# Dilated attention on one core: each compute engine's instructions issued in the order in which the program writes them

## The chip, the cores and the metric

The kernel runs on one core of one Trainium2 chip. Of the core's engines TensorE (PE in the profile) multiplies matrices and transposes, ScalarE (ACT), VectorE (DVE) and GpSimd (POOL) compute element by element, and SyncE (SP) issues most of the transfers between HBM and the on-chip memory SBUF. TensorE writes its results into PSUM, from where ScalarE and VectorE read them. Each engine takes its instructions from a queue of its own, in the order in which the compiler has put them there, and an instruction waits at the head of its queue until the semaphores that it names have been raised.

The metric is the device time of one execution of the program in microseconds (us), the median over runs. Lower is better.

## What is computed

The reference is two transformer blocks, one behind the other, over 2048 positions of width 1024. The change touches one stage of the first block, a dilated attention with 8 heads of width 64. Cut to what matters:

```python
DIL_PATTERNS = ((128, 1), (512, 4), (2048, 16))

def dilated_branch(q, k, v, slopes, window, dilation):
    r = window // (2 * dilation)
    ...
    s = jnp.einsum('bnqche,bnkche->bnchqk', qs, kw).astype(jnp.float32) * scale + bias
    s = jnp.where(mask, s, MASK_VALUE)
    m = jnp.max(s, axis=-1, keepdims=True)
    e = jnp.exp(s - m)
    l = jnp.sum(e, axis=-1, keepdims=True)
    o = jnp.einsum('bnchqk,bnkche->bnqche', e.astype(v.dtype), vw)
    ...
    return o, lse

def dilated_attention(q, k, v, slopes):
    outs, lses = [], []
    for window, dilation in DIL_PATTERNS:
        o, lse = dilated_branch(q, k, v, slopes, window, dilation)
        ...
    w = jax.nn.softmax(jnp.stack(lses, axis=0), axis=0)
    return jnp.sum(w[..., None] * jnp.stack(outs, axis=0), axis=0)
```

A query attends to the keys within 64 positions (the first pattern), and to keys at distances that are multiples of 4 and of 16 (the other two). The three results are merged by their softmax denominators.

## The kernel before

The program is a sequence of stages: the first projections (`phase_a`), a differential attention (`phase_b1`), the dilated attention (`phase_b2`), output projection and gate (`phase_c`), and the second block (`phase_d`, `phase_e`). The framework in which it is written takes the traced instructions with their dependencies, plays them through a timing model of its own, and so chooses for each engine an order of issue. Where several instructions are ready in that model, the one that the program writes first goes first. An instruction that the model takes to be ready can so be put ahead of one that the program wrote earlier.

`phase_b2` treats two kinds of tiles for each of the 8 heads, 16 tiles of 128 queries of each kind. A natural tile ("nat") holds neighbouring positions and does the first pattern against 256 keys. A residue tile ("res") holds positions of one residue modulo 4 and does the second and third pattern together, against 384 or 512 keys. One loop runs over `n` from 0 to 146. In each turn it writes pieces of several tiles, each at its own distance behind `n` (the constants `LB`, `LN`, `LEAD`, `DN`, `DR`). The order in which a turn writes them is this (the number of a piece's TensorE instructions in brackets):

- `scores_nat`, where `n` is even: scores of two nat tiles [4] (L563), VectorE adds the bias and takes the minimum, once for each tile (L566), ScalarE takes the exponential, once for each (L569)
- `scores_res`: scores of one res tile [2] (L590), VectorE (L593), ScalarE (L595)
- `trans_nat`, where `n` is odd: transposes [4] (L603), ScalarE copies them out of PSUM (L606), GpSimd splits them into a high and a low part (L610, L611)
- `trans_res`: transposes of a tile whose scores lie 4 turns back [3 or 4] (L622), ScalarE writes the high part (`d_ph`, L624), VectorE the low part (`d_pl`, L625), which reads what ScalarE wrote
- `back_nat`, where `n % 4 == 1`, and `back_res`, where `n % 4 == 3`: an attention output is transposed back [4] (L649), VectorE sums its two halves (L650)
- `pv_nat`, where `n % 4 == 0` [10] (L637), and `pv_res`, where `n % 4` is 1 or 2 [4 each] (L733): weights times values. ScalarE then copies the sum out of PSUM (`d_ta`, L643), at `n % 4 == 0` and `n % 4 == 2`

The res tiles of four turns have 512, 512, 384 and 384 keys, for `n % 4` of 0, 1, 2 and 3.

Once for each head some more is written. At `n = 16 h + 21` `back_nat` stores the head's nat results to HBM (L656, `d_o` to `s_o`) by a transfer on ScalarE's queue. At `n = 16 h + 33` `load_merge` loads them again in the order of the res tiles (L660, `s_o` to `d_a`), on ScalarE's queue too. It must wait until the store has landed. At `n = 16 h + 38` `weights` works out the merging factors from what was loaded: nine small VectorE instructions (L685 to L695, `d_mm` first) around two small ScalarE ones (L688, L689). For the last head these two come sooner. The merge itself goes to GpSimd piece by piece in the turns behind (`later`). `load_qk`, `load_vn`, `load_vr` and `double_k` fetch the operands of the next head, by SyncE's transfers, two ScalarE and some GpSimd instructions.

Of the kernel before, what the change touches and what calls it, by code (L numbers as in the profile page):

```python
# [1 line left out]

# [458 lines left out]
        rsqrt_dve(nc, fp, ssq, 128, ssq)  # L461


LB = 4
LN = 3
LEAD = 3
# [6 lines left out]
def phase_b2(tc, c, scr, nat_bias, res_bias, res_two):  # L473
    nc = tc.nc
    NS = 8 * NT
    with (
# [76 lines left out]
        def scores_nat(n):  # L553
            h, t = divmod(n, NT)
            q, k, _, _ = hd[h]
            if t == 0:
                o1s[h] = op1.tile([P, NT, 66], F32, name="d_o1")
            ml = o1s[h][:, t:t + 2, 64:66]
            ps = ps_n.tile([P, 2, 256], F32, name="d_sn")
            en = tp.tile([P, 2, 256], F32, name="d_en", bufs=3)  # L560
            for u in range(2):
                for i in range(2):
                    nc.tensor.matmul(ps[:, u], q[:, (t + u) * P:(t + u + 1) * P],  # L563
                                     k[i][:, (t + u) * P:(t + u) * P + 256], start=i == 0, stop=i == 1)
            for u in range(2):
                nc.vector.tensor_tensor_reduce(en[:, u], ps[:, u], nb[h % 2], 1.0, 3.0e38, ALU.add, ALU.min,  # L566
                                               ml[:, u, 0:1])
            for u in range(2):
                nc.scalar.activation(en[:, u], en[:, u], AF.Exp, bias=ml[:, u, 0:1], scale=-1.0,  # L569
                                     accum_out=ml[:, u, 1:2])  # L570
            en_[n] = en
# [5 lines left out]
        def scores_res(n):  # L577
            h, t = divmod(n, NT)
            q, k, _, _ = hd[h]
            if t == 0:  # L580
                m2s[h] = [sp.tile([P, NT], F32, name=nm, bufs=3) for nm in ("d_m2", "d_l2")]
            g4, s0 = divmod(t, 4)
            cls = 4 * s0 + g4
            m2, l2 = m2s[h][0][:, cls:cls + 1], m2s[h][1][:, cls:cls + 1]
            qr = q.rearrange("p (j r g) -> p j g r", r=P, g=4)[:, s0, g4]
            ps = ps_r.tile([P, 512], F32, name="d_sr")
            lo, hi = span(s0)
            for i in range(2):
                kr = k[i][:, 64:S + 64].rearrange("p (b g u) -> p g b u", g=4, u=16)[:, g4, lo // 16:hi // 16]
                nc.tensor.matmul(ps[:, lo:hi], qr, kr, start=i == 0, stop=i == 1)  # L590
            er = tp.tile([P, 512], F32, name="d_er")
            off = (3 - s0) * P
            nc.vector.tensor_tensor_reduce(er[:, lo:hi], ps[:, lo:hi], rb[h % 2][:, off + lo:off + hi], 1.0,  # L593
                                           3.0e38, ALU.add, ALU.min, m2)
            nc.scalar.activation(er[:, lo:hi], er[:, lo:hi], AF.Exp, bias=m2, scale=-1.0, accum_out=l2)  # L595
            er_[n] = er

        def trans_nat(n):
            en = en_.pop(n)
            pt = pt_n.tile([P, 2, 2, P], F32, name="d_tn")  # L600
            for u in range(2):
                for j in range(2):
                    nc.tensor.transpose(pt[:, u, j], en[:, u, j * P:(j + 1) * P], c["id"])  # L603
            t = n % 4
            pn = up.tile([P, 2, 2, P], F32, name="d_pn")
            nc.scalar.activation(pn, pt, AF.Copy)  # L606
            if t == 0:
                pn_[n // 4] = [pp.tile([P, 4, 2, P], F32R, name=nm) for nm in ("d_nh", "d_nl")]
            nh, nl = pn_[n // 4]
            nc.gpsimd.tensor_scalar(nh[:, t:t + 2], pn, 1.0, 1.0, ALU.mult, ALU.mult)  # L610
            nc.gpsimd.tensor_sub(nl[:, t:t + 2], pn, nh[:, t:t + 2].bitcast(F32))  # L611
# [45 lines left out]

        def load_merge(h):
            a1 = op.tile([P, NT, 66], F32, name="d_a1")
            nc.scalar.dma_start(a1.rearrange("r (j g) w -> r j (g w)", g=4),  # L660
                                scr["o1"][h].rearrange("(j r g) w -> r j (g w)", r=P, g=4))
            sz = op.tile([P, NT, 64], F32, name="d_sz")
            for j in range(4):
                nc.sync.dma_start(sz[:, 4 * j:4 * j + 4], by_rows(scr["sz"][:, 512 + 64 * h:576 + 64 * h], j))
            mrg[h] = [a1, sz]
# [9 lines left out]
        def weights(h):  # L675
            a1, sz = mrg.pop(h)
            o2 = o2s[h]
            m2, l2 = m2s.pop(h)
            m1, l1 = a1[:, :, 64], a1[:, :, 65]

            def small(nm):
                return sp.tile([P, NT], F32, name=nm, bufs=2)

            mm, d1, d2, ll, lt = (small(nm) for nm in ("d_mm", "d_d1", "d_d2", "d_ll", "d_lt"))
            nc.vector.tensor_tensor(mm, m1, m2, ALU.min)  # L685
            nc.vector.tensor_sub(d1, mm, m1)
            nc.vector.tensor_sub(d2, mm, m2)
            nc.scalar.activation(d1, d1, AF.Exp)  # L688
            nc.scalar.activation(d2, d2, AF.Exp)  # L689
            nc.vector.tensor_mul(ll, l1, d1)  # L690
            nc.vector.tensor_mul(lt, l2, d2)
            nc.vector.tensor_add(ll, ll, lt)
            nc.vector.reciprocal(ll, ll)
            nc.vector.tensor_mul(d1, d1, ll)
            nc.vector.tensor_mul(d2, d2, ll)  # L695
            av = a1[:, :, 0:64]
            sd = op.tile([P, NT, 64], F32, name="d_sd", tag="d_o2") if h == 7 else None
            hs = (slice(0, NT // 2), slice(NT // 2, NT))

            def scale(x, ap, w):  # L700
                nc.gpsimd.tensor_mul(ap[:, x], ap[:, x], w[:, x].unsqueeze(2).broadcast_to([P, NT // 2, 64]))

            if h == 7:
                nc.gpsimd.tensor_mul(sd, sz, d2.unsqueeze(2).broadcast_to([P, NT, 64]))
                nc.vector.tensor_mul(av, av, d1.unsqueeze(2).broadcast_to([P, NT, 64]))
                nc.vector.tensor_mul(av, av, sz)

                def tail():
                    nc.vector.tensor_mul(o2, o2, sd)
                    nc.vector.tensor_add(av, av, o2)  # L710
                    store_y(h, av)

                later.append(tail)
                return
            later.extend([
                *[lambda x=x: scale(x, av, d1) for x in hs],
                *[lambda x=x: scale(x, o2, d2) for x in hs],
                *[lambda x=x: nc.gpsimd.tensor_add(av[:, x], av[:, x], o2[:, x]) for x in hs],
                *[lambda x=x: nc.gpsimd.tensor_mul(av[:, x], av[:, x], sz[:, x]) for x in hs],
                lambda: store_y(h, av),  # L720
            ])
# [23 lines left out]
        for h in range(2):  # L745
            load_qk(h)
            load_vn(h)
            load_vr(h)
        for n in range(NS + LEAD + LB + 12):
            r = n - LEAD  # L750
            if n < NS and n % 2 == 0:
                scores_nat(n)
            if 0 <= r < NS:
                scores_res(r)
            m = n - LN
            if m % 2 == 0 and 0 <= m < NS:
                trans_nat(m)
            if 0 <= r - LB < NS:
                trans_res(r - LB)
            m = n - LN - DN  # L760
            if m % 4 == 0 and 0 <= m - 1 < NS:
                back_nat(m - 1)
            if m % 4 == 3 and 0 <= m < NS:
                pv_nat(m)
            for h in range(8):
                at = NT * (h + 1) + LN + DN + (BACK if h < 7 else 3)
                if n == at:
                    load_merge(h)
            m = r - LB - 4 - DR
            if 0 <= m and m % 4 == 2 and m < NS:  # L770
                back_res(m // NT, (m % NT) // 4)
            if 0 <= m < NS and m % 4 < 2:
                for kt in ((1, 2), (0, 3))[m % 4]:
                    pv_res(m // NT, (m % NT) // 4, kt)
            for h in range(8):
                if n == NT * (h + 1) + (WT if h < 7 else LEAD + LB + DR + 3):
                    weights(h)
            for f in later[:1 if n < NS else 2]:
                f()
            del later[:1 if n < NS else 2]  # L780
            h, t = divmod(n, NT)
            if 1 <= h < 7:
                if t == LEAD + 1:
                    load_qk(h + 1)
                if t == LN + DN + 1:
                    load_vn(h + 1)
                if t == LEAD + LB + DR + 2:
                    load_vr(h + 1)
                if t >= 8:
                    double_k(h + 1, t - 8)  # L790


def split_w(nc, dst, raw, gain=None, lo_eng=None):
# [580 lines left out]
```

## Time and profile before

| | |
|---|---|
| median of 3 runs | 3005.81 us (3000.62 to 3008.73) |
| the profiled execution, its own time | 2996.59 us |
| its span in the profile | 2994.8 us |
| mean granted TensorE clock | 0.985 |
| the stage that the change touches | from about 1320 to about 1712 us of the span |

The span is the time between the first and the last instruction of the profiled execution; its own time is 1.8 us longer. The granted clock is TensorE's clock as a share of 2.4 GHz; its two levels are 1.0 and 0.5 (2.4 and 1.2 GHz), and a number between them is a mean over a stretch.

### The profile page before, as it was taken

What the parts mean: (1) busy time and instruction counts of PE and PEld (TensorE: products, weight loads), DVE (VectorE), ACT (ScalarE), POOL (GpSimd) and SP (SyncE); (2) the same over time, 40 slices, a digit from 0 to 9 for tenths busy, and PEclk for the clock granted to TensorE, in tenths of its full rate; (3) what the DMA queues carried; (4) which work ended last, traced back from release to release, by engine and by line L of the source; (5) the groups of instructions that cost most, each with busy time, mean ns of one, the idle gap of its engine ahead of it and who ended that gap; (6) DMA issues with size and microseconds to landing.
All of it is one profiled execution on the core that took longest, in us unless ns stands there. A gap on an engine that the chain in (4) does not pass through costs nothing.

```text
span 2994.8 us, 45167 instructions
## 1 busy us (share of the span) xinstructions
PE 2891.2 (97%) x15554; PEld 2464.7 (82%) x15554; DVE 1802.8 (60%) x4607; ACT 1565.5 (52%) x3480; POOL 1240.2 (41%) x1156
## 2 busy tenths in 40 slices
PE   9999999999999999998898899999999999999998
PEld 7778888888788888888787778888788888888787
DVE  4115656522788889877676654444535756766755
ACT  5222333311688888877787642222345666666621
POOL 1110111101688888845676610000145665555421
PEclk9999999999999999999999899999999999999999
DMA  6653444414223322148666452322554343332452
GB/s 211 118 155 85 120 114 120 112 65 142 91 56 90 82 60 77 44 110 166 131 144 126 126 159 83 111 93 92 183 162 153 98 132 110 101 117 71 142 192 78
DMA packets 410645, 346.00 MB, mean 116 GB/s; under 512 B 89744, under 2 KB 356400, under 8 KB 408496
## 3 DMA queue, kind: packets, MB, share of 16 engines
q1 hardware_dynamic: 388000, 329.24, 39.3%
q10 hardware_dynamic: 20736, 8.65, 1.5%
q0 software_dynamic: 1680, 5.21, 0.7%
q8 instruction: 124, 2.03, 0.3%
q14 instruction: 105, 0.86, 0.1%
HBM read 227.51 MB, written 116.52 MB: 115 GB/s over the span
## 4 chain that ended last, share of the span: by engine, by line
PE 85%; DMA 6%; DVE 3%; ACT 2%; SPq 1%; issue 1%; POOL 1%; ACTq 0%; DVEq 0%; POOLq 0%
PE psm L190 8%; PE psm L192 8%; PE psm L191 8%; PE s_ps L331 7%; PE e_mm L803 5%; PE e_mm L805 5%; PE e_mm L804 5%; PE c_mm L803 4%; PE c_mm L804 4%; PE c_mm L805 4%; PE t_ps L375 3%; DMA s_o<-d_o 2%; PE o_ps L389 2%; PE o_ps L391 2%; PE o_ps L390 2%; PE f_mm L804 2%
## 5 line engine op out<-in xcount | busy, mean ns | idle before, releaser
L190 PE MATMUL psm<-w,hh 128*128 128x512 f32 x1024 | 406.1, 398 | 9.8 <-DVE t L111 8.0
L191 PE MATMUL psm<-w,hl 128*128 128x512 f32 x1024 | 399.9, 392 | 0.0
L192 PE MATMUL psm<-w,hh 128*128 128x512 f32 x1024 | 399.8, 393 | 0.0
L101 POOL TENSOR_TENSOR w<-wraw,w 128x512 fp32r<-128x512 f32 x64 | 81.7, 1296 | 599.0 <-ACT w L100 591.2
L365 POOL TENSOR_TENSOR et<-et 128x1024 f32<-128x1024 f32 x124 | 296.4, 2416 | 0.0
L331 PE MATMUL s_ps<-kst,qst 128*128 128x512 f32 x1024 | 289.3, 406 | 4.6 <-DVE mx L337 3.6
L347 ACT ACTIVATE et<-et,nm 128x2048 f32<-128x2048 f32 x128 | 257.3, 2010 | 5.2
L1025 POOL TENSOR_TENSOR e_wt<-e_raw,e_wt 128x1024 fp32r<-128x1024 f32 x80 | 191.3, 2399 | 111.5 <-ACT e_wt L1024 110.6
L190 PEld LDWEIGHTS psm<-w,hh 128*128 128x128 f32 x1024 | 193.5, 189 | 48.6 <-DVE t L111 8.4
L803 PE MATMUL e_mm<-e_x,e_wt 128*128 128x512 f32 x576 | 228.2, 396 | 1.1 <-DVE e_k L1067 0.9
L805 PE MATMUL e_mm<-e_x,e_wt 128*128 128x512 f32 x576 | 226.9, 394 | 0.0
L192 PEld LDWEIGHTS psm<-w,hh 128*128 128x128 f32 x1024 | 193.1, 189 | 40.8
L804 PE MATMUL e_mm<-e_x,e_wt 128*128 128x512 f32 x576 | 226.6, 393 | 0.0
L191 PEld LDWEIGHTS psm<-w,hl 128*128 128x128 f32 x1024 | 193.7, 189 | 38.3
L331 PEld LDWEIGHTS s_ps<-kst,qst 128*128 128x128 f32 x1024 | 176.2, 190 | 43.8 <-DVE mx L337 17.7
L1126 POOL TENSOR_SCALAR e_es<-e_es,e_l 128x256 f32<-128x256 f32 (+1 forms) x256 | 118.4, 481 | 170.6 <-DVE e_l L1124 108.5
L364 POOL TENSOR_SCALAR et<-et,cc 128x1024 f32<-128x1024 f32 x124 | 138.6, 1134 | 109.2 <-PE psm L192 57.1
L377 DVE TENSOR_TENSOR ptl<-t_ps,pth 128x512 fp32r<-128x512 f32 x256 | 169.2, 684 | 17.6 <-ACT pth L376 17.1
L337 DVE CUSTOM_DVE_ANT_0 et<-s_ps,nd,mx 128x1024 f32<-128x1024 f32 x128 | 163.8, 1280 | 26.5 <-PE s_ps L331 24.6
L1113 DVE CUSTOM_DVE_ANT_0 e_es<-e_s,e_bias,e_sk 128x256 f32<-128x256 f32 (+1 forms) x256 | 117.4, 472 | 102.7 <-PE e_s L1105 71.3
L376 ACT ACTIVATE pth<-t_ps 128x512 fp32r<-128x512 f32 x256 | 143.8, 596 | 42.7 <-PE t_ps L375 39.0
L337 DVE CUSTOM_DVE_ANT_0 et<-s_ps,nd 128x1024 f32<-128x1024 f32 x128 | 156.1, 1219 | 14.3 <-PE s_ps L331 7.0
(268 smaller groups left out, 7727.6 us busy)
## 6 DMA issues: line engine op xcount, KB each, us to landing
e_raw<-in_a_w_in_dram SPq DMA_DIRECT2D x80, 512.0 KB, 3.6
wraw<-in_w_in_dram SPq DMA_DIRECT2D x64, 256.0 KB, 3.5
kst<-s_dk SPq DMA_DIRECT2D x128, 128.0 KB, 4.0
s_xt<-c_at SPq DMA_DIRECT2D x32, 512.0 KB, 6.9
e_x<-s_xt SPq DMA_DIRECT2D x32, 512.0 KB, 7.7
t<-in_x_dram SPq DMA_DIRECT2D x32, 256.0 KB, 5.6
s_dv<-t SPq DMA_DIRECT2D x32, 256.0 KB, 3.2
s_bv<-t SPq DMA_DIRECT2D x32, 256.0 KB, 3.7
```

What stands on the lines that cost most here:

```text
L190: nc.tensor.matmul(ps, ah, cur[k][:, 0], start=k == 0, stop=False)
L191: nc.tensor.matmul(ps, al, cur[k][:, 0], start=False, stop=False)
L192: nc.tensor.matmul(ps, ah, cur[k][:, 1], start=False, stop=k == KD - 1)
L331: nc.tensor.matmul(ps[:, b * 512:b * 512 + 512], lhs, heads[h, "k", e, i, 2 * hf + b], start=i == 0, stop=i == 1)
L337: nc.vector.tensor_tensor_reduce(et[:, hf], ps, bias[:, off:off + 1024], 1.0, -3.0e38 if hf == 0 else mx[:, 0:1], ALU.add, ALU.max, mx[:, ...
L347: nc.scalar.activation(ev, ev, AF.Exp, bias=nm, scale=slope, accum_out=st[g]["l"][:, e:e + 1])
L365: nc.gpsimd.tensor_sub(es[0][:, hf], es[0][:, hf], es[1][:, hf])
L377: nc.vector.tensor_sub(tl[:, :, qi], pt, th[:, :, qi].bitcast(F32))
L803: nc.tensor.matmul(ps, ah, bh, start=first, stop=False)
L804: nc.tensor.matmul(ps, al, bh, start=False, stop=False)
L805: nc.tensor.matmul(ps, ah, bl, start=False, stop=last)
L1025: nc.gpsimd.tensor_sub(w[:, 1], raw, w[:, 0].bitcast(F32))
```

## The change

The loop of `phase_b2` is put into a context `in_order`. When the loop has been traced, it goes through all instructions that were traced inside, and gives each instruction of TensorE, ScalarE, VectorE and GpSimd an edge from the one that was traced before it on the same engine. The edge carries no semaphore: it binds the order of issue alone. Transfers that ScalarE and GpSimd issue are bound with their engine; those of SyncE are not. Two instructions get a second pin of the same kind, behind all that was traced on their engine before them: the load of `load_merge` (L660) and the first instruction of `weights` (L685). What is computed stays the same, and so does every buffer.

```diff
+@contextmanager
+def in_order(tc, *engines):
+
+    made = tc.nc.cur_bb.bb.instructions
+    seen = {id(i) for i in made}
+    yield
+    last = {}
+    for i in made:
+        if id(i) in seen or i.engine not in engines:
+            continue
+        if i.engine in last:
+            tc.add_manual_dep(
+                i, last[i.engine].name,
+                mybir.DependencyInfo(mybir.DependencyClass.NoSync, mybir.DependencyReason.DATA), reason="in_order")
+        last[i.engine] = i
...
         def load_merge(h):
             a1 = op.tile([P, NT, 66], F32, name="d_a1")
-            nc.scalar.dma_start(a1.rearrange("r (j g) w -> r j (g w)", g=4),
-                                scr["o1"][h].rearrange("(j r g) w -> r j (g w)", r=P, g=4))
+            tc.keep_in_program_order(nc.scalar.dma_start(
+                a1.rearrange("r (j g) w -> r j (g w)", g=4),
+                scr["o1"][h].rearrange("(j r g) w -> r j (g w)", r=P, g=4)))
...
-            nc.vector.tensor_tensor(mm, m1, m2, ALU.min)
+            tc.keep_in_program_order(nc.vector.tensor_tensor(mm, m1, m2, ALU.min))
...
-        for n in range(NS + LEAD + LB + 12):
-            r = n - LEAD
...
+        eng = mybir.EngineType
+        with in_order(tc, eng.PE, eng.Activation, eng.DVE, eng.Pool):
+            for n in range(NS + LEAD + LB + 12):
+                r = n - LEAD
...
```

The body of the loop is unchanged but for its indentation.

## Rows read from the trace of the kernel before

**Rows 1.** The page's first lines: span, and TensorE's busy time and instructions.
```profile
span 2994.8 us, 45167 instructions
...
PE 2891.2 (97%) x15554; PEld 2464.7 (82%) x15554; DVE 1802.8 (60%) x4607; ACT 1565.5 (52%) x3480; POOL 1240.2 (41%) x1156
```

**Rows 2.** Busy time in three stretches: from:to, length, engines (x instructions), clock, DMA.
```profile
1580.00:1590.00 10.00, 5.42 (x25) 4.53 (x25) 2.98 (x15) 5.46 (x19) 3.87 (x5) 0.83 0.28 63
1640.00:1650.00 10.00, 10.00 (x74) 9.67 (x73) 8.18 (x27) 9.90 (x31) 10.00 (x11) 1.00 0.01 2
1650.00:1660.00 10.00, 10.00 (x70) 9.54 (x70) 8.13 (x26) 9.20 (x27) 7.60 (x9) 1.00 0.44 106
```

**Rows 3.** Line L656, the store of a head: ns min/median/max, first and last start.
```profile
L656 ACTq DMA_DIRECT2D s_o<-d_o x8: 366/366/436, 1387.0 to 1700.4; - x8
```

**Rows 4.** Timeline at a head's end: start, length, engine, line, [idle before <- releaser].
```profile
1572.06 0.37 ACTq L656 DMA_DIRECT2D s_o<-d_o  x1
...
1583.68 0.72 ACT L595 ACTIVATE d_er<-d_er,d_m 128x512 f32<-128x512 f32 x1 [5.43 <-DMA s_o<-d_o]
...
1586.91 0.18 DVE L685 TENSOR_TENSOR d_mm<-d_a,d_m 128x16 f32<-128x16 f32 x1 [6.88 <-DMA d_a<-s_o]
```

**Rows 5.** Instruction groups by shape, 1320 to 1715: busy us, mean ns | idle.
```profile
L569 ACT ACTIVATE d_en<-d_en,d_o 128x256 f32<-128x256 f32 x128 | 64.0, 504 | 1.7 <-DVE d_o L566 1.6
L595 ACT ACTIVATE d_er<-d_er,d_m 128x512 f32<-128x512 f32 x64 | 46.2, 722 | 13.4 <-DMA s_o<-d_o 10.8 <-DVE d_m L593 2.5
L650 DVE TENSOR_REDUCE d_o<-d_ob 128x256 f32<-128x512 f32 x64 | 43.8, 684 | 17.5 <-PE d_ob L649 17.3
L625 DVE TENSOR_TENSOR d_pl<-d_tr,d_ph 128x512 fp32r<-128x512 f32 x64 | 43.7, 683 | 7.3 <-ACT d_ph L624 7.2
L595 ACT ACTIVATE d_er<-d_er,d_m 128x384 f32<-128x384 f32 x64 | 39.3, 614 | 1.4 <-DVE d_m L593 1.3
...
L606 ACT ACTIVATE d_pn<-d_tn 128x512 f32<-128x512 f32 x64 | 38.0, 593 | 6.4 <-PE d_tn L603 4.7 <-POOL d_nl L611 1.5
L624 ACT ACTIVATE d_ph<-d_tr 128x512 fp32r<-128x512 f32 x64 | 37.9, 593 | 12.9 <-DMA s_o<-d_o 6.0 <-PE d_tr L622 5.9 <-PE d_tn L603 0.8
L625 DVE TENSOR_TENSOR d_pl<-d_tr,d_ph 128x384 fp32r<-128x384 f32 x64 | 35.2, 549 | 10.6 <-ACT d_ph L624 10.4
L624 ACT ACTIVATE d_ph<-d_tr 128x384 fp32r<-128x384 f32 x64 | 31.1, 486 | 12.7 <-DMA s_o<-d_o 6.5 <-PE d_tr L622 5.4 <-PE d_or L733 0.5
...
L566 DVE CUSTOM_DVE_ANT_0 d_en<-d_sn,d_nb__13769 128x256 f32<-128x256 f32 x64 | 24.6, 421 | 11.5 <-PE d_sn L563 5.2 <-PE d_tn L603 5.0 <-ACT b_an L414 0.9
...
L593 DVE CUSTOM_DVE_ANT_0 d_er<-d_sr,d_rb__13771 128x512 f32<-128x512 f32 x32 | 21.9, 688 | 8.6 <-PE d_tr L622 7.5 <-PE d_sr L590 0.6
...
L593 DVE CUSTOM_DVE_ANT_0 d_er<-d_sr,d_rb__13772 128x384 f32<-128x384 f32 x32 | 17.8, 555 | 6.7 <-PE d_tr L622 6.7
...
L692 DVE TENSOR_TENSOR d_ll<-d_ll,d_lt 128x16 f32<-128x16 f32 x8 | 3.6, 453 | 0.1
```

**Rows 6.** Timeline of ScalarE and VectorE, 1592.3 to 1593.5, where both have work.
```profile
1592.30 0.62 ACT L624 ACTIVATE d_ph<-d_tr 128x512 fp32r<-128x512 f32 x1
...
1592.78 0.53 ACT L569 ACTIVATE d_en<-d_en,d_o 128x256 f32<-128x256 f32 x1
...
1592.85 0.68 DVE L650 TENSOR_REDUCE d_o<-d_ob 128x256 f32<-128x512 f32 x1
...
1593.27 0.64 ACT L595 ACTIVATE d_er<-d_er,d_m 128x384 f32<-128x384 f32 x1
1593.45 0.68 DVE L625 TENSOR_TENSOR d_pl<-d_tr,d_ph 128x512 fp32r<-128x512 f32 x1
```

**Rows 7.** Timeline in the last head's `weights`, where each waits for the other.
```profile
1711.78 0.19 DVE L686 TENSOR_TENSOR d_d<-d_mm,d_a 128x16 f32<-128x16 f32 x1
...
1712.00 0.22 ACT L688 ACTIVATE d_d<-d_d 128x16 f32<-128x16 f32 x1 [4.45 <-DVE d_d L686]
...
1712.25 0.18 DVE L690 TENSOR_TENSOR d_ll<-d_a,d_d 128x16 f32<-128x16 f32 x1 [0.20 <-ACT d_d L688]
```

More of the change, by code (lines that the diff above doesn't have):

```diff
@@ L1 @@
-from contextlib import nullcontext
+from contextlib import contextmanager, nullcontext
 import concourse.bass as bass
@@ L748, in phase_b2 @@
             load_vr(h)
-        for n in range(NS + LEAD + LB + 12):
-            r = n - LEAD
[L751 to L790, printed above, removed]
@@ new lines, in phase_b2 @@
+        eng = mybir.EngineType
+        with in_order(tc, eng.PE, eng.Activation, eng.DVE, eng.Pool):
+            for n in range(NS + LEAD + LB + 12):
+                r = n - LEAD
+                if n < NS and n % 2 == 0:
+                    scores_nat(n)
+                if 0 <= r < NS:
+                    scores_res(r)
+                m = n - LN
+                if m % 2 == 0 and 0 <= m < NS:
+                    trans_nat(m)
+                if 0 <= r - LB < NS:
+                    trans_res(r - LB)
+                m = n - LN - DN
+                if m % 4 == 0 and 0 <= m - 1 < NS:
+                    back_nat(m - 1)
+                if m % 4 == 3 and 0 <= m < NS:
+                    pv_nat(m)
+                for h in range(8):
+                    at = NT * (h + 1) + LN + DN + (BACK if h < 7 else 3)
+                    if n == at:
+                        load_merge(h)
+                m = r - LB - 4 - DR
+                if 0 <= m and m % 4 == 2 and m < NS:
+                    back_res(m // NT, (m % NT) // 4)
+                if 0 <= m < NS and m % 4 < 2:
+                    for kt in ((1, 2), (0, 3))[m % 4]:
+                        pv_res(m // NT, (m % NT) // 4, kt)
+                for h in range(8):
+                    if n == NT * (h + 1) + (WT if h < 7 else LEAD + LB + DR + 3):
+                        weights(h)
+                for f in later[:1 if n < NS else 2]:
+                    f()
+                del later[:1 if n < NS else 2]
+                h, t = divmod(n, NT)
+                if 1 <= h < 7:
+                    if t == LEAD + 1:
+                        load_qk(h + 1)
+                    if t == LN + DN + 1:
+                        load_vn(h + 1)
+                    if t == LEAD + LB + DR + 2:
+                        load_vr(h + 1)
+                    if t >= 8:
+                        double_k(h + 1, t - 8)
```

## The prediction

> **What bounds the kernel now.** I read the page first: TensorE is busy for 97% of the span [rows 1], so over the whole program it is the engine that sets the time. The change touches only the dilated stage, so I went on to busy time by stretches of 10 us inside it. Two kinds of stretch alternate there [rows 2]. In a dense one all four compute engines are at work: TensorE full, ScalarE at 9.2 and 9.9 of 10, VectorE at 8.1 and 8.2, and 74 and 70 matmuls run, 7.2 per us. In a stretch at the end of a head 25 matmuls run, TensorE is busy for 5.4 of 10 us and its clock is granted at 0.83.
>
> The timeline shows what happens at such an end [rows 4]. The store of a head is issued at 1572.06 from ScalarE's queue. The load that reads it back has been put so early in the same queue that ScalarE stands behind it until the store has landed (5.43 us of idle time, next instruction at 1583.68, 11.6 us after the store), and VectorE stands for 6.88 us in front of the first instruction of `weights`, which needs the load. TensorE starves a little later.
>
> The line of the store gives the pace [rows 3]: eight stores between 1387.0 and 1700.4, so seven heads in 313.4 us, 44.8 us per head, 2.80 us per turn of `n`, ends of heads included.
>
> **What the change removes.** In the written order 12 turns lie between store and load, and 5 between load and `weights`. Even at the old pace 12 turns are 33.6 us, against 11.6 us for the store, and 5 turns are 14 us, against 3.2 us from the end of ScalarE's wait to the first instruction of `weights` [rows 4]. Both waits go, but for the last head's. I price the gain at the difference between a stretch at an end and a dense one: 10 - 5.4 = 4.6 us of TensorE and 0.17 of 10 us of clock, so some 6.3 us per head, 44 us in all. It is not added to the sum below, since that counts the new pace from its parts; it is what a rival would keep.
>
> **What it adds.** Program order makes ScalarE and VectorE wait for each other in every turn. In a turn VectorE handles scores (L566, L593), then the low part `d_pl` (L625), then, in odd turns, the sum of halves (L650). ScalarE does exponentials (L569, L595), then the copy L606 in odd turns, then the high part `d_ph` (L624). The low part needs this turn's high part. The next turn's exponentials need scores that now stand behind this low part on VectorE. So there is one closed chain: low part, sum, scores, exponentials, copy, high part, and the next turn's low part. No buffer loosens it, for it runs through the queues themselves. Before, the two engines did not keep to it: in rows 6 VectorE takes a sum of halves and a low part while ScalarE goes from a high part to exponentials that were ready already.
>
> Durations are means by shape [rows 5]. Where an instruction follows another on its engine, it starts a little before the other's end [rows 6]: the low part at 1593.45 starts 0.60 us after a sum of 0.68, an exponential 0.48 us after a high part of 0.62, the next 0.49 us after one of 0.53. So I take 0.08 us off on VectorE and 0.11 us off ScalarE's copies, 0.02 off its exponentials, but nothing where the other engine must wait for the end. A handover from engine to engine takes 0.03 us both ways [rows 7]: L686 ends at 1711.97, L688 starts at 1712.00; that ends at 1712.22, L690 starts at 1712.25.
>
> The four turns, each from the end of a high part to the end of the next, in us:
>
> - into `n % 4 == 0`: low part (384) 0.47, sum 0.60, first score tile 0.42, two exponentials 0.98, res exponential (512) 0.70, high part 0.59, two handovers 0.06: 3.82
> - into 1: low part (512) 0.60, res scores (512) 0.69, exponential 0.70, copy 0.48, high part 0.59, 0.06: 3.12
> - into 2: low part (512) 0.60, sum 0.60, score tile 0.42, exponentials 0.98, res exponential (384) 0.60, high part (384) 0.49, 0.06: 3.75
> - into 3: low part (384) 0.47, res scores (384) 0.55, exponential 0.60, copy 0.48, high part 0.49, 0.06: 2.65
>
> Together 13.34 us for four turns, 3.34 per turn, 53.4 per head, against 44.8 now, stalls included.
>
> **What hides elsewhere.** ScalarE's evacuation `d_ta` costs nothing on this chain: it runs while VectorE does the low part and the scores. TensorE needs 64 matmuls for four turns, 64 / 7.2 = 8.9 us, so it has 4.4 us to spare; it may run ahead until the next `back_nat` or `back_res`, which waits for `d_ta` of the turn before, and that is far enough for the next scores. If its cover went, the price is the rival on the clock below. GpSimd is full only in the dense stretch where the merge falls [rows 2], its splits have three turns until `pv_nat`, and at a slower pace it gains room. SyncE's transfers are not bound, and a slower head gives them more time.
>
> **Once per head.** `weights` now stands in the chain: nine small VectorE instructions, from 0.18 us (L690 in rows 7) to a mean of 0.45 us (L692 in rows 5), with ScalarE's two between them. Below, nothing, if all of them fell into waits; above, 9 x 0.45 = 4.1 us. VectorE is what the chain waits for at that point, so it is not nothing; I take 2.5 us. The two pinned transfers fall where ScalarE has free time before the next score tile, and cost nothing; if that were wrong, each is 0.37 us [rows 4].
>
> **The sum.** Between the first store (`n` = 21) and the last (`n` = 133) lie 106 full turns, 106 x 3.34 = 354 us, and six of the emptying loop, which I put at 12 us from the same parts (no score tiles any more, then no exponentials), and seven `weights`, 17.5 us: 383.5 us against 313.4 [rows 3], so +70. The 14 turns before the first store, from the first low part on, lose 14 x (3.34 - 2.80) = 7.6 us. The tail behind the last store does not change: there the load waits for the store in either order, with nothing left to overlap. Sum: +78 us. The profiled execution of 2996.6 us (span 2994.8, rows 1) would become 3074.6. The median of the runs lies 9.2 us above that execution, so the forecast is 3005.8 + 78 = 3084 us.
>
> Bounds: without handovers (10 us), without `weights` (17.5 us) and with a few us that the next stage can prepare in the new gaps, +45 us, 3050. With 4.1 us per `weights` (+11) and a clock that falls for a third of the time (below, +44), +133 us, 3139. The forecast's own range is 3050 to 3140.
>
> **The rivals.**
>
> *TensorE's clock falls (slower still).* TensorE would be at work for 8.9 of 13.34 us. For it: the granted clock is 0.83 in the stretch with 5.4 us of work [rows 2]. Against it: there the idle time was in one piece, while here it comes in pieces of under 2 us, because every turn brings TensorE work. At 1.2 GHz 8.9 us become at most 17.8, which is 4.4 us more than the chain, 30 groups of four turns, +133 us: 3217 if it held all through, about 3150 for half of it. The Trainium skill speaks for this rival: "TensorE: Matmul & The Clock Gate", section "A second HAM failure mode: psum-queue depth-cycling", reports a kernel in which short idle times of TensorE between groups of matmuls made the clock swing between half and full. By that page the forecast would be some 3150 us; no row here shows a swing with gaps so short, and I stay with 3084.
>
> *The engines keep overlapping (faster).* The place is VectorE's queue. Had ScalarE enough finished scores in front of it to go on while VectorE does the low part, each head would run at the dense pace, 256 matmuls / 7.2 = 35.6 us, and seven heads would save 7 x 9.2 = 64 us: 2942 us. It decides as soon as a turn takes less than 2.80 us. For it: the stalls at heads' ends do go. Against it: the chain above would have to be 16% shorter than its own durations.
>
> *Only the two pins act (faster).* If the compiler's order inside the loop were kept and only the load and `weights` moved, the 44 us stay as gain: 2962 us. Against it: the edges are made between all instructions of the four engines.
>
> *Nothing changes.* That would need an issue order that is the written one already. Against it: the load stands directly behind the store [rows 4], and VectorE goes from a sum to a low part [rows 6], where the written order has scores.
>
> **How the numbers follow.** Forecast 0.80, clock rival 0.10, overlap 0.05, only the pins 0.03, nothing 0.02. A difference under 0.3% (9 us) is what a measurement of this kernel can't tell from no change. Slower is the first two, less 0.01 for a chain that the removed waits just pay for: 0.89. Faster 0.08, the same 0.03. The range 3045 to 3150 holds the forecast's own range and half of the clock rival, and leaves out the faster cases.
>
> **What would show it.** In the profile of the changed kernel: the stores 55 to 57 us apart in place of 44.8; no wait of VectorE for `s_o` but for the last head; ScalarE's longest waits at L569 and L595, for VectorE's scores, and VectorE's at L625, for the high part, hundreds of short ones; TensorE at 60 to 70% in this stage with a clock near 1.0; L688 and L690 waiting for each other once per head. The prediction is wrong if stores come less than 45 us apart, if TensorE stays full in the stage, or if the granted clock there lies under 0.9.

## The result and the profile after

The changed kernel takes 3087.24 us (median of 4 runs, 3084.01 to 3088.58), the kernel before 3005.94 us beside it (median of 4). The ratio is 1.0271, with a 95% interval of 1.0253 to 1.0289: slower by 81 us. The forecast was 3084 us.

Lines from the head of the page, which answer to [rows 1]:

```profile
span 3086.4 us, 45120 instructions
...
PE 2905.7 (94%) x15554; PEld 2469.1 (80%) x15554; DVE 1805.3 (58%) x4607; ACT 1566.0 (51%) x3480; POOL 1241.0 (40%) x1156
```

The engines have nearly as much to do as before: TensorE 14.5 us more, the others at most 2.5 us. The span has grown by 91.6 us, so most of what was added is waiting. Busy time of three stretches inside the stage, with the columns of [rows 2]:

```profile
1400.00:1500.00 100.00, 78.56 (x479) 71.29 (x478) 54.39 (x171) 64.29 (x181) 50.62 (x59) 0.92 0.48 105
1500.00:1600.00 100.00, 74.22 (x453) 67.23 (x454) 54.41 (x174) 64.91 (x180) 61.20 (x70) 0.93 0.52 101
1600.00:1700.00 100.00, 75.51 (x463) 68.69 (x462) 53.71 (x175) 65.11 (x180) 55.93 (x63) 0.93 0.58 117
```

No engine is full any more: TensorE 74 to 79%, ScalarE 64 to 65%, VectorE 54%. The dense stretches of [rows 2], with TensorE full and 70 or 74 matmuls in 10 us, are gone: of the 43 stretches of 10 us from 1350 to 1780 us none has TensorE full, and none has more than 59 matmuls. The store of a head, which was L656 in [rows 3], is L673 now:

```profile
L673 ACTq DMA_DIRECT2D s_o<-d_o x8: 366/366/383, 1396.0 to 1780.2; - x8
```

Eight stores in 384.2 us, 54.9 us per head in place of 44.8. Who waited for whom, from 1320 to 1790 us (total us, times, longest):

```profile
DVE d_pl L642 <- ACT d_ph L641: 189.0, 123, 2.5
...
PE d_ob L666 <- ACT d_ta L660: 105.6, 63, 3.5
ACT d_en L586 <- DVE d_o L583: 96.1, 58, 2.9
ACT d_er L612 <- DVE d_m L610: 48.7, 55, 1.8
...
ACT d_ta L660 <- DMA s_o<-d_o: 5.8, 1, 5.8
```

VectorE's low part waits for ScalarE's high part in nearly every turn, 123 times of 128. ScalarE's exponentials wait for VectorE's scores, 58 times at the nat and 55 times at the res tiles. That is the closed chain, seen from both sides. The wait for `s_o` of [rows 4] is gone, but for the last head's (5.8 us). Four turns of the chain in the timeline of VectorE and ScalarE, from one low part (384 keys) to the one that has the same place four turns on:

```profile
1568.19 0.56 DVE L642 TENSOR_TENSOR d_pl<-d_tr,d_ph 128x384 fp32r<-128x384 f32 x1 [1.64 <-ACT d_ph L641]
1568.67 0.68 DVE L667 TENSOR_REDUCE d_o<-d_ob 128x256 f32<-128x512 f32 x1
1569.27 0.41 DVE L583 CUSTOM_DVE_ANT_0 d_en<-d_sn,d_nb__13769 128x256 f32<-128x256 f32 x1
...
1569.72 0.51 ACT L586 ACTIVATE d_en<-d_en,d_o 128x256 f32<-128x256 f32 x1 [1.56 <-DVE d_o L583]
...
1570.73 0.70 ACT L612 ACTIVATE d_er<-d_er,d_m 128x512 f32<-128x512 f32 x1
...
1571.43 0.57 ACT L641 ACTIVATE d_ph<-d_tr 128x512 fp32r<-128x512 f32 x1
...
1572.03 0.69 DVE L642 TENSOR_TENSOR d_pl<-d_tr,d_ph 128x512 fp32r<-128x512 f32 x1 [1.39 <-ACT d_ph L641]
...
1575.18 0.69 DVE L642 TENSOR_TENSOR d_pl<-d_tr,d_ph 128x512 fp32r<-128x512 f32 x1 [1.85 <-ACT d_ph L641]
...
1578.94 0.56 DVE L642 TENSOR_TENSOR d_pl<-d_tr,d_ph 128x384 fp32r<-128x384 f32 x1 [1.31 <-ACT d_ph L641]
...
1581.61 0.56 DVE L642 TENSOR_TENSOR d_pl<-d_tr,d_ph 128x384 fp32r<-128x384 f32 x1 [1.64 <-ACT d_ph L641]
```

Each low part starts 0.03 to 0.04 us after the high part has ended, and while VectorE goes through low part, sum and first scores ScalarE stands still for 1.56 us. From one low part to the next the turns take 3.84, 3.15, 3.76 and 2.67 us, 13.42 together. The prediction worked out 3.82, 3.12, 3.75 and 2.65.

### The profile page after: what moved, and what is told of

Same layout as the page of the kernel before. It is cut to its first block, busy times and chain, and to the rows that moved or that the text cites. A ratio compares the mean times of both kernels' runs of the same rounds, so it can differ in the third digit from the quotient of the medians.

```text
span 3086.4 us, 45120 instructions
## 1 busy us (share of the span) xinstructions
PE 2905.7 (94%) x15554; PEld 2469.1 (80%) x15554; DVE 1805.3 (58%) x4607; ACT 1566.0 (51%) x3480; POOL 1241.0 (40%) x1156
## 5 line engine op out<-in xcount | busy, mean ns | idle before, releaser
L642 DVE TENSOR_TENSOR d_pl<-d_tr,d_ph 128x384 fp32r<-128x384 f32 (+1 forms) x128 | 79.9, 624 | 189.0 <-ACT d_ph L641 189.0
```

## The experiments

Ten kernels ran, each beside the kernel before, whose median was 2997.69 to 2999.66 us there. So they are compared by their ratio to it. Edits are against the changed kernel unless another is named.

**Only the two pins.** The edges of the loop are left out.

```diff
-        with in_order(tc, eng.PE, eng.Activation, eng.DVE, eng.Pool):
+        with in_order(tc):
```

> The edges inside the loop are left out; only the load of load_merge and the first instruction of weights stay pinned. Theory: the loss of the change comes from the order inside the turns (the closed chain of VectorE and ScalarE), and the pins alone give back the waits at the heads' ends, about 44 us: 2962 us, stores about 39 us apart, no wait of VectorE for s_o but in the last head. Rival: the waits at the heads' ends were hidden work put elsewhere, and the pins change nothing: within 9 us of 3006.

Measured: 2958.13 us, ratio 0.9871 (0.9856 to 0.9886). The store in its trace:

```profile
L673 ACTq DMA_DIRECT2D s_o<-d_o x8: 366/366/385, 1387.4 to 1661.5; - x8
```

39.2 us per head, as expected. VectorE's waits for the load are gone but for the last head's (3.8 us). So the change has two parts of opposite sign: the pins give 1.3%, 39 us, and the order of the turns takes 4.0% (1.0271 - 0.9871), some 120 us. This kernel is the fastest of all and beats both the one before and the changed one.

**Which pin.** From the kernel with the two pins, one is taken off.

```diff
 pin_load:
-            tc.keep_in_program_order(nc.vector.tensor_tensor(mm, m1, m2, ALU.min))
+            nc.vector.tensor_tensor(mm, m1, m2, ALU.min)
 pin_first:
-            tc.keep_in_program_order(nc.scalar.dma_start(
+            nc.scalar.dma_start(
```

> No edges in the loop, and of the two pins only that of the load in load_merge. Theory: ScalarE no longer stands behind the store, but VectorE's first instruction of weights may still be put ahead of the load's landing, so a wait of up to 5 us per head stays there: 2960 to 2990 us. Rival: the load's place was all of the loss: 2958 us as with both pins.

> No edges in the loop, and of the two pins only that of the first instruction of weights. Theory: the load stands early on ScalarE's queue as before and ScalarE waits some 5 us per head for the store, while VectorE's wait is gone: 2975 to 3000 us. Rival: VectorE's wait was all of the loss: 2958 us as with both pins.

Measured: the load alone 2962.23 us, ratio 0.9871 (0.9851 to 0.9891); the first instruction of `weights` alone 2983.90 us, ratio 0.9953 (0.9937 to 0.997). The pin of the load does all that both do. My theory for it was half right: VectorE's wait did stay, from 1330 to 1790 us in its trace,

```profile
DVE d_mm L703 <- DMA d_a<-s_o: 15.8, 8, 3.9
```

but it costs nothing that the ratio shows. The stores of this one trace are 40.2 us apart (1387.6 to 1668.8 us) against 39.2, so up to 1 us per head may be left of it. The rival holds as far as the times can tell: with the load in its place nothing more is gained. With the other pin alone about a third of the gain comes, within the 2975 to 3000 us expected, though ScalarE still stands seven times for the store, 37.1 us in all. So VectorE's wait cost something too while the load stood too early, and the two gains do not add up.

**One engine free.** Three kernels leave the edges of one engine out, and keep those of the other three.

```diff
 free_act:
+        with in_order(tc, eng.PE, eng.DVE, eng.Pool):
 free_dve:
+        with in_order(tc, eng.PE, eng.Activation, eng.Pool):
 free_pe:
+        with in_order(tc, eng.Activation, eng.DVE, eng.Pool):
```

> As the changed kernel, but ScalarE's instructions are left without edges (TensorE, VectorE and GpSimd stay in written order). Theory: the chain is closed only if both queues hold to the written order; with ScalarE free, the high part of a turn can be put ahead of its exponentials, VectorE no longer waits for it, and the time falls to 2950 to 3010 us. Rival: binding the engines costs in proportion, so two thirds of the loss stay: 3060 us or more.

> As the changed kernel, but VectorE's instructions are left without edges (TensorE, ScalarE and GpSimd stay in written order). Theory: with VectorE free the next turn's scores can be put ahead of the low part, the chain opens, and the time falls to 2950 to 3010 us. Rival: binding the engines costs in proportion: 3060 us or more.

> As the changed kernel, but TensorE's instructions are left without edges (ScalarE, VectorE and GpSimd stay in written order). Theory: the closed chain runs through ScalarE's and VectorE's queues alone, so freeing TensorE gives back nothing: ratio to the kernel before 1.024 to 1.030, stores 54 to 56 us apart. Rival: TensorE's waits for d_ta, the longest of TensorE in the changed kernel (105.6 us), are a part of the cause, and freeing it gives back as much as freeing ScalarE or VectorE did: ratio near 1.00.

Measured: ScalarE free 2990.96 us, ratio 0.9983 (0.9971 to 0.9994); VectorE free 3000.23 us, ratio 1.0012 (1.0002 to 1.0022); TensorE free 3088.63 us, ratio 1.0295 (1.0278 to 1.0312). To free either of the two engines of the chain takes away 2.6 to 2.9 of the 4.0%; 1.1 to 1.4% stay. To free TensorE takes away nothing. Most of the loss is not spread over the bound engines; it is in the pair. GpSimd was not freed by itself. The trace of the kernel with TensorE free, its store, the two waits and one stretch of busy time:

```profile
L673 ACTq DMA_DIRECT2D s_o<-d_o x8: 366/367/383, 1398.8 to 1782.4; - x8
```

```profile
DVE d_pl L642 <- ACT d_ph L641: 191.9, 127, 2.0
...
PE d_ob L666 <- ACT d_ta L660: 58.5, 63, 2.6
```

```profile
1500.00:1600.00 100.00, 79.11 (x462) 66.72 (x461) 55.54 (x180) 64.25 (x179) 61.69 (x71) 0.97 0.47 101
```

TensorE's waits for `d_ta` have nearly halved (105.6 to 58.5 us) and its clock has gone from 0.93 to 0.97, yet a head still takes 54.8 us, and VectorE waits for the high part as long as in the changed kernel. The long waits of this engine, which is not on the chain, are worth nothing here. With ScalarE free the same wait of VectorE (1330 to 1690 us, and the same from 1320 to 1790) is down from 189.0, though not gone:

```profile
DVE d_pl L642 <- ACT d_ph L641: 82.0, 62, 4.8
```

**The chain opened in written order.** All four engines stay bound, but the program writes the low part behind the next turn's scores.

```diff
-            nc.vector.tensor_sub(pl[:, ka:kb, s0], pt[:, ka:kb], ph[:, ka:kb, s0].bitcast(F32))
+            low.append(lambda: nc.vector.tensor_sub(pl[:, ka:kb, s0], pt[:, ka:kb], ph[:, ka:kb, s0].bitcast(F32)))
...
                 if 0 <= r < NS:
                     scores_res(r)
+                if low:
+                    low.pop(0)()
```

> As the changed kernel, all four engines in written order, but the program writes the low part of a turn behind the next turn's scores in place of behind its own high part. Theory: the chain from high part to high part then takes two turns in place of one, so it allows 13.3 us for about eight turns and no longer binds; the pace is set by ScalarE's and TensorE's own work, 9.5 to 10.5 us for four turns, 40 to 44 us per head: 2975 us, at most 3010. Rival: it is written order as such that costs (TensorE's queue waiting at back_nat and back_res), and the time stays above 3060 us.

Measured: 2989.78 us, ratio 0.9976 (0.9967 to 0.9986). Its store, and two of its waits (1330 to 1690 us; the second is the same from 1320 to 1790):

```profile
L673 ACTq DMA_DIRECT2D s_o<-d_o x8: 366/366/384, 1387.0 to 1686.3; - x8
```

```profile
PE d_ob L666 <- ACT d_ta L660: 30.3, 36, 4.7
...
DVE d_pl L642 <- ACT d_ph L641: 5.0, 2, 4.4
```

A head takes 42.8 us, and VectorE's wait for the high part has fallen from 189 to 5 us. One moved line takes back 3.0 of the 4.0%, in an order that is still bound on every engine. So most of the loss is this one dependence, and not written order as such. 1.05% (32 us) remain against the kernel with the pins alone.

**The remainder.** The same edit, and TensorE's edges left out.

> As late_low (low part written behind the next turn's scores), and TensorE left without edges. Theory: with the chain opened, what keeps late_low 32 us above the kernel with the two pins alone is TensorE's queue in written order, which stands at back_nat and back_res for d_ta; freed, the time falls to a ratio of 0.985 to 0.992. Rival: the rest lies in ScalarE's and VectorE's order still, and the ratio stays at 0.997.

Measured: 2974.95 us, ratio 0.9916 (0.9902 to 0.9931), and 41.6 us per head by the stores:

```profile
L673 ACTq DMA_DIRECT2D s_o<-d_o x8: 366/367/379, 1383.8 to 1674.7; - x8
```

Once the chain is open, TensorE's queue does cost: 0.6 of the remaining 1.05%. The other 0.45% (14 us) I did not follow further; GpSimd, ScalarE and VectorE are still bound there.

**A dose on the chain and one beside it.** ScalarE has two copies out of PSUM that are equally long and equally many, 64 each: L606 (`d_pn`), which by the prediction lies on the chain, and the evacuation `d_ta`, which lies beside it. Each is made twice in one kernel.

```diff
 twice_pn:
             nc.scalar.activation(pn, pt, AF.Copy)
+            nc.scalar.activation(pn, pt, AF.Copy)
 twice_ta:
             nc.scalar.activation(ta, po, AF.Copy)
+            nc.scalar.activation(ta, po, AF.Copy)
```

> The changed kernel with ScalarE's copy L606 (d_pn, out of PSUM) made twice in each odd turn; the second copy writes the same values again. Theory: this copy lies on the closed chain, so each of the 64 second copies costs its full 0.48 us: 64 x 0.48 = 31 us, 3118 us. Rival: ScalarE is busy for only 65 of 100 us in this stage, so the copies fall into its idle time and the time stays at 3087 us.

> The changed kernel with ScalarE's evacuation d_ta (out of PSUM, behind the attention matmuls) made twice; the second copy writes the same values again. It is as long as d_pn and there are as many, 64. Theory: it runs while VectorE does the low part and the scores, where ScalarE waits anyway (0.9 and 0.6 us left), so it costs next to nothing: 3087 to 3093 us. Rival: ScalarE's own load sets the pace, and it costs as much as the doubled d_pn: 3118 us.

Measured: `d_pn` twice 3128.81 us, ratio 1.0432 (1.041 to 1.0454); `d_ta` twice 3093.49 us, ratio 1.0314 (1.0297 to 1.0331). Their stores, `d_pn` first:

```profile
L674 ACTq DMA_DIRECT2D s_o<-d_o x8: 366/366/384, 1400.9 to 1819.8; - x8
```

```profile
L674 ACTq DMA_DIRECT2D s_o<-d_o x8: 365/366/384, 1396.7 to 1786.2; - x8
```

Between first and last store lie 54 of the second copies of `d_pn` and 56 of those of `d_ta`. The one on the chain lengthens the stretch from 384.2 to 418.9 us, 0.64 us per copy; the one beside it to 389.5, 0.09 us per copy. The rivals fall: ScalarE's idle time does not take up a copy as such, it depends on where the idle time lies. Both doses came out above what was expected. The price on the chain was sized too low, at 0.48 us. The timeline with `d_pn` twice shows why:

```profile
1578.07 0.58 ACT L623 ACTIVATE d_pn<-d_tn 128x512 f32<-128x512 f32 x1
1578.68 0.60 ACT L624 ACTIVATE d_pn<-d_tn 128x512 f32<-128x512 f32 x1
1579.18 0.59 ACT L642 ACTIVATE d_ph<-d_tr 128x512 fp32r<-128x512 f32 x1
```

The second copy writes what the first wrote and starts only 0.03 us after its end, 0.61 us behind its start. The high part, which has nothing to do with it, follows after 0.50 us. By the profiled spans the two doses cost 37.4 us (3123.8) and 3.0 us (3089.4); by the ratios 48 and 13 us, with intervals of some 10 us either way. The gap between the two is shown by both; the last 10 us of either are not settled, nor whether the copy beside the chain costs the 0 to 6 us expected or twice that.

## Why the prediction was right, and where it was not

**The chain** was the main term, and it holds to 1%: 13.42 us for four turns against 13.34. That it sets the pace of the changed kernel, and makes some three quarters of what the order costs, is shown by `late_low` and by the kernels with one engine free; the last quarter shows only once the chain is open. That no buffer loosens it was argued and not tried, but a line in another place does.

**From first to last store** the sum gave 383.5 us, measured 384.2. Inside it errors cancel, and that is luck. The chain took 355.6 us (106 x 3.355) in place of 354. `weights` was set at seven times 2.5 us on the chain. The turn that holds it, from low part to low part:

```profile
1452.71 0.56 DVE L642 TENSOR_TENSOR d_pl<-d_tr,d_ph 128x384 fp32r<-128x384 f32 x1 [1.66 <-ACT d_ph L641]
1453.19 0.17 DVE L703 TENSOR_TENSOR d_mm<-d_a,d_m 128x16 f32<-128x16 f32 x1
...
1453.62 0.22 ACT L706 ACTIVATE d_d<-d_d 128x16 f32<-128x16 f32 x1 [0.45 <-DVE d_d L704]
...
1453.86 0.18 DVE L708 TENSOR_TENSOR d_ll<-d_a,d_d 128x16 f32<-128x16 f32 x1 [0.20 <-ACT d_d L706]
...
1454.86 0.55 DVE L610 CUSTOM_DVE_ANT_0 d_er<-d_sr,d_rb__13771 128x384 f32<-128x384 f32 x1
...
1457.05 0.56 DVE L642 TENSOR_TENSOR d_pl<-d_tr,d_ph 128x384 fp32r<-128x384 f32 x1 [1.64 <-ACT d_ph L641]
```

It takes 4.34 us, the same turn without `weights` 2.67 (1578.94 to 1581.61 above): 1.67 us each. And only six lie in this stretch: `weights` is written at `n` = 38, 54 and so on up to 134, and the last store at 133. So it is 10.0 us in place of 17.5. The mean of 0.45 us that I leaned on [rows 5] has instructions of up to 1.26 us in it, with a median of 0.24; here each takes 0.17 to 0.26 us.

The rest of the stretch, 384.2 - 355.6 - 10.0 = 18.6 us, was more than the 12 us allowed for the emptying loop. That loop was sized nearly right: its six turns took 13.1 us from low part to low part. Some 3.9 us more went into the three turns ahead of it, where work for the next stage stands between the bound instructions (L815 on ScalarE, L816 on VectorE). The longest of them:

```profile
1756.86 0.69 DVE L642 TENSOR_TENSOR d_pl<-d_tr,d_ph 128x512 fp32r<-128x512 f32 x1 [2.53 <-ACT d_ph L641]
...
1759.23 3.67 DVE L816 TENSOR_TENSOR c_wo<-c_raw,c_wo 128x512 fp32r<-128x512 f32 x2
...
1762.82 0.54 DVE L642 TENSOR_TENSOR d_pl<-d_tr,d_ph 128x384 fp32r<-128x384 f32 x1
```

This turn takes 5.96 us in place of 3.76. The edges hold the loop's instructions to one another and let others in between; the prediction had counted what the next stage prepares in the gaps as a gain alone.

**The turns before the first store** were to lose 7.6 us; the first store moved from 1387.0 to 1396.0, by 9.0.

**The tail behind the last store** is the step that failed. The prediction said that it does not change. The store of the last merged results, before (L672) and after (L690):

```profile
L672 POOL DMA_DIRECT2D s_y<-d_a x32: 692/767/973, 1416.9 to 1728.9; - x32
```

```profile
L690 POOL DMA_DIRECT2D s_y<-d_a x32: 714/804/1022, 1480.9 to 1815.4; - x32
```

The last of them is issued 28.5 us behind the last `d_o` store before (1700.4), and 35.2 us behind it after (1780.2): 6.7 us later in the written order. From that last `d_o` store to the span's end the profiled executions take 1294.4 and 1306.2 us, 11.8 us more. The traces show where the 6.7 us arise. The last head's `weights` on VectorE, first and last instruction, before and then after, with one instruction behind it:

```profile
1711.56 0.18 DVE L685 TENSOR_TENSOR d_mm<-d_a,d_m 128x16 f32<-128x16 f32 x1 [7.06 <-DMA d_a<-s_o]
...
1715.72 0.17 DVE L695 TENSOR_TENSOR d_d<-d_d,d_ll 128x16 f32<-128x16 f32 x1
```

```profile
1791.90 0.17 DVE L703 TENSOR_TENSOR d_mm<-d_a,d_m 128x16 f32<-128x16 f32 x1
...
1798.86 0.16 DVE L713 TENSOR_TENSOR d_d<-d_d,d_ll 128x16 f32<-128x16 f32 x1
...
1800.12 5.43 DVE L816 TENSOR_TENSOR c_wo<-c_raw,c_wo 128x512 fp32r<-128x512 f32 x1
```

From the store to its first instruction it is 0.5 us more than before (11.7 against 11.2 us), within `weights` 2.8 us (7.1 against 4.3), and from there to the last transfer 3.4 us (16.4 against 13.0). So the wait for the landing of the store was seen nearly rightly, and what was left out is the work behind it. Instructions for the next stage stand between on VectorE in both kernels; the longest there takes 5.43 us after and 1.77 us before. The order has a part in it: the last transfer is issued 27.3 to 29.0 us behind the last store in the four kernels without edges in the loop (the one before among them), and 31.6 to 35.5 us in the eight with edges. Which instruction of the order does it was not tried. The other 5.1 us lie behind that transfer, where it is 1265.9 us to the end before and 1271.0 after, and 1265.5 to 1270.6 in the ten other traces, so no cause can be given for them.

**The base.** The profiled spans differ by 91.6 us, the medians by 81.3. The profiled execution of before lay 9.2 us under the median of its first three runs; that of after lies 1.0 us over its own. The forecast took the difference from one execution and put it on the median. So the closeness of 3084 to 3087.24 owes something to chance: the missed tail (11.8 us) and the low base offset each other. The lower bound took 10 us off for the handovers, where 120 turns of 0.06 us make 7.2; nothing hangs on it.

**The gain of the pins**, which I priced at 44 us without adding it, measured 39 us. Its cause was given rightly for the load; the wait of VectorE, named with it, adds nothing measurable once the load is in its place.

**TensorE and its clock.** TensorE had its room, as said: freeing it changed nothing. But its idle times were not under 2 us: the waits at `d_ob` reach 3.5 us, and the granted clock was 0.92 to 0.93 in the stage, a mean over its two levels, and not near 1.0. It had been 0.95 from 1400 to 1700 us before, so it hardly fell. TensorE was busy for 74 to 79%, not 60 to 70. The Trainium skill ("TensorE: Matmul & The Clock Gate", section "A second HAM failure mode: psum-queue depth-cycling") has the clock swing in a kernel with frequent short idle times. The trace agrees: between 1400 and 1750 us the granted clock of stretches of 10 us lies between 0.83 and 1.00. What the rival made of it does not follow: `free_pe` ran at 0.97 and took as long.

**The rivals.** The engines did not overlap on (a turn took 3.36 us, far over 2.80), and the edges acted. One reading in them was loose: the load did not stand directly behind the store, since ScalarE worked on to 1578.25 us before it stood still (1583.68 less 5.43, [rows 4]).

## What to carry to other kernels

When two engines hand work to each other within a turn, follow the order of issue through both queues and look for a path that comes back to its start within one turn; here its sum gave the turn's time to 1%, with no engine over 79% busy. This chain was opened by writing the returning step behind the next turn's first step, and a copy added on it cost 0.64 us, one beside it 0.09 us. Pin single instructions that a compiler puts too early, above all a transfer that must wait for another, before binding whole engines.

## What the runs showed of the hardware that was not expected

On ScalarE a copy that overwrites the copy ahead of it starts 0.61 us behind that one's start (0.60 to 0.64 in the pairs of both doses), an unrelated one 0.48 to 0.50 us behind: rewriting a tile cost 0.13 us beyond the instruction itself. Whether the engine or a wait set by the program does this was not tried. VectorE's nine small instructions of `weights` took 0.16 to 0.26 us each in the changed kernel but for the last head, where four of them took 0.70 to 1.28 us; in the kernel before the same operations ranged from 0.15 to 1.27 us, with the same operands. Which of the engines beside it slowed them was not tried.
